# Zero rows and columns around a hybrid decoder step's small matrix products, and one exponent matrix per delta head

## The chip, the cores and the metric

The kernel runs on one core of one Trainium2 chip. The time is the device time of one execution, in microseconds (us); before the change it is 2520.16, the median of three runs (2520.1 to 2521.52).

## The reference

Two decoder layers run for a prompt of 512 tokens and for 8 samples of 8 new tokens each, with the same weights. Each layer projects the normalised input once, gives the columns to three branches, merges them by sigmoid gates, projects again, adds the residual, and ends with a gated MLP. The branches are HGRN2 (a gated linear recurrence), differential attention, and the gated delta rule. The delta rule is the one whose algebra the change touches; per chunk and head it is

```python
G = jnp.cumsum(gc, axis=-1)
D = jnp.exp(jnp.where(incl, G[..., :, None] - G[..., None, :], -jnp.inf))
KK = jnp.einsum('bhtd,bhsd->bhts', kc, kc)
A = jnp.where(strict, bc[..., :, None] * D * KK, 0.0)
eg = jnp.exp(G)[..., None]
rhs = bc[..., None] * (vc - eg * jnp.einsum('bhtd,bhdv->bhtv', kc, S))
U = lax.linalg.triangular_solve(A, rhs, left_side=True, lower=True, unit_diagonal=True)
QK = jnp.einsum('bhtd,bhsd->bhts', qc, kc) * D
o = eg * jnp.einsum('bhtd,bhdv->bhtv', qc, S) + jnp.einsum('bhts,bhsv->bhtv', QK, U)
S = jnp.exp(GL)[..., None, None] * S + jnp.einsum('bhsd,bhsv->bhdv', kc * jnp.exp(GL[..., None] - G)[..., None], U)
```

with `q`, `k` normalised to length 1 per token (and `q` divided by the root of 128), `b` the beta of a token, and an RMS norm of `o` over the head's 128 values behind it.

## The kernel before

All 576 tokens (512 of the prompt, 64 of the samples, `NS`) lie along the free dimension, 128 channels along the partitions. A projection's tile of 128 output channels is made by `dense_steps` (line 265): for each 128 input channels six products of 128x288 in the fp32r type (weight high with input high and low, weight low with input high, over two halves of the tokens). These big products accumulate in two PSUM tiles `acc`. For one output tile (`wide=True`, line 1420, the first output projection of layer 0) the halves are 512 and 64 tokens instead.

Everything else on TensorE is small: fp32 products (each shown as two instructions, two passes) and transposes (one instruction) of 128 tokens at a time, made by `mm` (line 180) and `trp` (line 190) into tiles of the pool `psR`, which has four PSUM banks and is shared by all heads (`rp`, line 169). The samples' 64 tokens are a fifth block, and most products on it have 64 rows or 64 columns of the array.

The order of the work is planned when the program is made. `drive` (line 319) keeps three lanes (left, right, samples). Each lane runs one head at a time as a Python generator; `yield win(i)` asks for a projection tile, `yield 0.7` lets the lane sleep for so long by a clock `clk` to which each product adds an assumed cost. Between the lanes' steps `drive` issues the big products of the next tile. The instructions of an engine then run in the order in which the program stands, except that one whose inputs come late in the framework's own plan may have been put behind others.

A delta head (`gdn_head`, line 752; 4 per layer) does the following. Convolution and SiLU of the keys and queries into `ckq` (`conv_silu`), transposition of the keys into `kt`, sums of squares `ss`. `parts(i)` splits an exponent per token into three bf16 parts `pc`; `weights(i, pc)` transposes them (15 columns), spreads them over the array with five selector products on 15 rows (`sel`, `rt`), adds the other exponent `w1` and a mask, takes the exponential into `dd`, and multiplies it into the products of keys with keys (i = 0) or keys with queries (i = 1), giving `ap[:, i]` for the prompt and `aps[:, i]` for the samples. `weights(0)` is called at line 835, the solve of the 16x16 diagonal blocks follows on VectorE with two round trips through DRAM and ends in `TB` and `TS`; after `yield 4.5` (line 886) comes `weights(1)`, then `yield 11.0` (line 907), and then products of `ap[:, 0]` and `TB` that build the whole inverse. The chunk loop makes `R`, `U` and the state `S`; the samples' part makes `Rs` and `Us` with 64x64 products. `sample_state` and `finish_gated` end the head; the latter uses `head_norm` and `transpose_back`.

`hgrn_head` (line 990) makes its matrix by levels m = 1, 2, ..., 64 (`level`, line 1026); for m up to 4 each has a product for the samples on 64 columns. Its samples' output starts with the 64x64 product of `ATs`. `diff_head` and `qk_prep` use `transpose_to` (line 470) and `transpose_back` (line 485); `diff_sample` multiplies the weights `PT` by past values and, for the samples' own tokens, by `Vs` on 64 rows.

Of the kernel before, what the change touches and what calls it, by code (L numbers as in the profile page):

```python
# [28 lines left out]
HALF = T // 2  # L29
PAST = 1024  # L30
# [115 lines left out]
def kernel(ctx, tc, a, o, depth=DEPTH, dbg=None):  # L146
# [118 lines left out]
    def dense_steps(src, xs, M=128, raws=None, nk=None, prime=False, wide=False):  # L265
# [23 lines left out]
        for g, (k0, n) in enumerate(gr):  # L289
            wh, wl = nxt  # L290
            for i in range(n):
                if i == min(1, n - 1) and g + 1 < len(gr):
                    nxt = weights(g + 1)
                xh, xl = xs[k]
                cs = slice(i * M, (i + 1) * M)
                for w, xx in ((wh, (xh, xl)), (wl, (xh,))):
                    for hf in range(2):
                        for x_ in xx:
                            ts = (slice(0, SEQ), slice(SEQ, T))[hf] if wide else slice(hf * HALF, (hf + 1) * HALF)
                            mm(acc[:M, hf, :ts.stop - ts.start], w[:, cs], x_[:, ts],  # L300
                               start=(k == 0 and w is wh and x_ is xh), stop=(k == nk - 1 and w is wl))
                k += 1
                if k < nk:
                    yield
        if wide:
            return acc.rearrange('p a b -> p (a b)')[:, 0:T].rearrange('p (a b) -> p a b', a=2)
        return acc[:, :, :HALF]

    def dense(src, xs, wide=False):
        return run(dense_steps(src, xs, wide=wide))  # L310
# [159 lines left out]
    def transpose_to(dst, src, scale=None):  # L470
# [4 lines left out]
        trp(ps2[:NS, 0:128], src[:, SEQ:], ident)  # L475
        G.memset(dst[NS:, 4, :], 0.0)
        if scale is None:
            S.copy(dst[:, 0:4, :], ps.rearrange('p (j d) -> p j d', j=4))
            S.copy(dst[:NS, 4, :], ps2[:NS, 0:128])
# [3 lines left out]
        S.activation(dst[:NS, 4, :], ps2[:NS, 0:128], AF.Copy, scale=scale[:NS, 4:5])  # L483

    def transpose_back(src):
# [18 lines left out]
    def finish_gated(ot, key, src, gcol, dst, p, tag):  # L504
# [3 lines left out]
        head_norm(ot, p)  # L508
# [128 lines left out]
    for l in range(depth):  # L637
# [10 lines left out]
        bh = lay.tile([128, 5, 4], F32, tag='bh', name='bh')  # L648
# [4 lines left out]
        GB = lay.tile([128, 5, 4], F32, tag='GB', name='GB')  # L653
        GC = lay.tile([128, 5, 4], F32, tag='GC', name='GC')
# [19 lines left out]
        def decays(p):  # L674
# [9 lines left out]
            S.activation(bh, sp[:, :, 0:4], AF.Exp, scale=-1.0)  # L684
            V.tensor_scalar(out=bh, in0=bh, scalar1=0.5, scalar2=None, op0=ALU.mult)
# [3 lines left out]
            lab = lay.tile([NS, NB, 4], F32, tag='lab', name='lab')  # L689
            tt(lab, bc1(la[:NS, 4, :], NB), bc(c['bm8'][:NS], 4), ALU.mult)  # L690
# [4 lines left out]
            mm(ps[:, 32:64], ones[:NS, :], lab.rearrange('p b e -> p (b e)'))  # L695
            mm(ps[:NS, 64:68], c['trib'][:NS], la[:NS, 4, :])
            mm(ps[:NS, 68:72], c['oneb'][:NS], la[:NS, 4, :])
# [6 lines left out]
            tt(GB, Gt, sp[:, :, 0:4], ALU.subtract)  # L704
            V.tensor_scalar(out=GC, in0=Gt, scalar1=-0.5 * math.log(128.0), scalar2=None, op0=ALU.add)
            V.tensor_scalar(out=nG, in0=Gt, scalar1=-1.0, scalar2=None, op0=ALU.mult)
# [45 lines left out]
        def gdn_head(h, p):  # L752
            ckq = p.tile([128, 2, T], F32, tag='ckq', name='ckq')
            cv = p.tile([128, T], F32, tag='hn', name='cv')
            sel = c['sel'].rearrange('p (j t) -> p j t', j=5)
            mad = c['madd'].rearrange('p (a t) -> p a t', a=2)
            mads = c['madds'].rearrange('p (a t) -> p a t', a=2)
            conv_silu((yield win(4 * h + 0)), 4 + h, ckq[:, 0])
# [5 lines left out]
            aps = p.tile([NS, 2, NS], F32, name='aps')  # L764
# [6 lines left out]
            trp(ps2[:NS, 0:128], ckq[:, 0, SEQ:], ident)  # L771
            S.copy(kt[:, 0:4], ps.rearrange('p (j t) -> p j t', j=4))
            S.copy(kt[:NS, 4], ps2[:NS, 0:128])
# [5 lines left out]
            u2 = sm.tile([128, 2, 5], F32, tag='u2', name='u2')  # L779
            V.scalar_tensor_tensor(out=u2[:, 0], in0=ss[:, 0], scalar=-0.5, in1=GB[:, :, h], op0=ALU.mult, op1=ALU.add)  # L780
# [3 lines left out]
            def parts(i):  # L784

                pc = sm.tile([128, 3, 5], BF16, tag='pc', name='pc')
                rr = sm.tile([128, 5], F32, tag='rr', name='rr')
                V.tensor_copy(pc[:, 0], u2[:, i])
                tt(rr, u2[:, i], pc[:, 0], ALU.subtract)
# [3 lines left out]
                return pc  # L793

            def weights(i, pc):
# [4 lines left out]
                V.tensor_copy(rt, pst[:15, 0:128])  # L800
                yield 0.7
                pb, pg = rp(), rp()
                for j in range(4):
                    cs = slice(128 * j, 128 * j + 128)
                    mm(pb[:, cs], sel[:15, j, :], rt)
                    mm(pg[:, cs], ckq[:, 0, cs], ckq[:, i, cs])
                dd = p.tile([128, 4, 128], F32, tag='x5', bufs=2, name='dd')
                for j in range(4):
                    V.scalar_tensor_tensor(out=dd[:, j], in0=pb[:, 128 * j:128 * j + 128], scalar=w1[:, j:j + 1], in1=mad[:, i],
                                           op0=ALU.add, op1=ALU.add)  # L810
                if i:
                    S.activation(eq[:, 0:SEQ], pb, AF.Exp)
# [5 lines left out]
                if i:  # L818
                    S.activation(eq[:, SEQ:], pb[:, 0:NS], AF.Exp)
                dds = p.tile([NS, 4, 16], F32, tag='dds', name='dds')  # L820
                dv = dds.rearrange('p j t -> p (j t)')
                V.scalar_tensor_tensor(out=dv, in0=pb[:NS, 0:NS], scalar=w1[:NS, 4:5], in1=mads[:NS, i], op0=ALU.add, op1=ALU.add)
                S.activation(dv, dv, AF.Exp)
                tt(aps[:, i], pb[:NS, 128:128 + NS], dv, ALU.mult)

            pc = parts(0)
            conv_silu(acc, h, ckq[:, 1])
            ex = sm.tile([128, 2, 5], F32, tag='ex', name='ex')
            V.tensor_copy(ex[:, 0], u2[:, 0])
# [5 lines left out]
            yield from weights(0, pc)  # L835
# [9 lines left out]
            tt(xts, aps[:, 0].rearrange('p (j t) -> p j t', j=4), bc(bm[:NS, 0:4], 16), ALU.mult)  # L845
# [20 lines left out]
            TS = p.tile([NS, 2, 4, 16], F32, name='TS')  # L866
            for i in range(2):
                for cc in range(4):
                    tt(TB[:, i, cc].rearrange('p (j t) -> p j t', j=8), bc1(ct[:, i, cc], 8), bc(bm, 16), ALU.mult)
                tt(TS[:, i], bc1(ct[:NS, i, 4], 4), bc(bm[:NS, 0:4], 16), ALU.mult)  # L870

            conv_silu(acc, 8 + h, cv)
            yield 1.0
            ps, ps2 = rp(), rp()
            for j in range(5):
                n = 128 if j < 4 else NS
                pj = ps[:, 128 * j:128 * j + 128] if j < 4 else ps2[:NS, 0:128]
                trp(pj, ckq[:, 1, 128 * j:128 * j + n], ident)
                ks = p.tile([128, 128], F32, tag='U', bufs=2, name='ks')
                S.activation(ks[:n], pj, AF.Square, accum_out=ss[:n, 1, j:j + 1])  # L880
            S.activation(ss[:, 1], ss[:, 1], AF.Ln, bias=b4e)
            V.scalar_tensor_tensor(out=u2[:, 1], in0=ss[:, 1], scalar=-0.5, in1=GC[:, :, h], op0=ALU.mult, op1=ALU.add)
            pc = parts(1)
# [731 lines left out]
```

## Time and profile before

| | |
|---|---|
| median of three runs | 2520.16 us |
| profiled execution, device time | 2517.85 us |
| its span, first to last instruction | 2516.1 us |
| TensorE busy with products | 2492.3 us (99%) |
| TensorE busy with weight loads | 2338.6 us (93%) |
| VectorE busy | 1677.5 us (67%) |
| ScalarE busy | 1134.2 us (45%) |
| GpSimd busy | 119.3 us (5%) |
| granted TensorE clock, mean | 0.999 |
| products on TensorE | 19714 |

The times of instructions come from one execution, the profiled one. In the page and the timeline a product is written `out<-moving,stationary`, then the rows and columns of the array that it takes (`64*128` is 64 rows and 128 columns), then its input's form. `r` is a tile of the pool `psR`, `acc` the accumulator of a big product, `cf` the constants (for a transpose, the identity). Products are pipelined: a row's duration reaches from its start to its end, and the next product starts well before that end.

### The profile page before, as it was taken

Reading aid. Unit: us, or ns where it says so; the run is one execution under the profiler, and the core shown is the slowest. Engines: PE = TensorE matmul, PEld = TensorE weight load, DVE = VectorE, ACT = ScalarE, POOL = GpSimd, SP = SyncE. Lnnn points to the kernel's source line nnn. Section 1 sums busy time; section 2 is a strip of 40 time slices with the busy share of each in tenths; the row PEclk is TensorE's granted clock in tenths of the full one; section 3 lists DMA queues with packets and bytes.
Section 4 is the critical chain, followed back from the end, with each engine's and each line's share of the span. In section 5 each row is a group of like instructions: output and inputs, shape, how many; then the busy total and the mean of one; then the engine's idle time right before and its main releaser. Section 6 shows DMA issues by size and latency. Waiting matters only on the chain.

```text
span 2516.1 us, 52047 instructions
## 1 busy us (share of the span) xinstructions
PE 2492.3 (99%) x19714; PEld 2338.6 (93%) x19714; DVE 1677.5 (67%) x4218; ACT 1134.2 (45%) x2435; POOL 119.3 (5%) x378
## 2 busy tenths in 40 slices
PE   8999999999999999999999999999999999999999
PEld 7898888888899999999998988888889999999999
DVE  7777777777765663646676877777686656636463
ACT  5556555556433332323455565646464333323232
POOL 1000000000000010101000000000000000101010
PEclk9999999999999999999999999999999999999999
DMA  6233464545365324242432235554534653242423
GB/s 206 88 109 120 141 202 133 181 156 177 104 213 173 133 85 159 85 146 95 137 130 95 96 121 181 168 176 148 180 129 160 192 176 119 86 159 82 159 85 124
DMA packets 222843, 352.93 MB, mean 140 GB/s; under 512 B 36864, under 2 KB 71680, under 8 KB 222592
## 3 DMA queue, kind: packets, MB, share of 16 engines
q1 hardware_dynamic: 221008, 346.78, 42.3%
q8 instruction: 156, 2.56, 0.4%
q10 hardware_dynamic: 1584, 2.82, 0.4%
q14 instruction: 95, 0.78, 0.1%
HBM read 288.90 MB, written 60.60 MB: 139 GB/s over the span
## 4 chain that ended last, share of the span: by engine, by line
PE 93%; DVE 4%; ACT 2%; issue 1%; DMA 0%; SPq 0%; ACTq 0%; DVEq 0%
PE acc L188 75%; PE r L188 14%; PE r L192 4%; DVE mx L1216 1%; DVE wl L195 0%; ACT P L1219 0%; DVE r L195 0%; DMA x<-in_xT 0%; DVE mx L1289 0%; DMA pg<-in_v 0%; ACT ks L777 0%; DVE ca L743 0%; DVE thb L723 0%; DVE xl L427 0%; DVE ro L195 0%
## 5 line engine op out<-in xcount | busy, mean ns | idle before, releaser
L188 PE MATMUL acc<-xh,wh 128*128 128x288 f32 x3584 | 1026.1, 301 | 2.9 <-DVE thb L710 1.6
L188 PE MATMUL acc<-xl,wh 128*128 128x288 f32 x3584 | 1010.7, 297 | 1.0 <-DVE xl L427 0.9
L188 PE MATMUL acc<-xh,wl 128*128 128x288 f32 x3584 | 773.3, 296 | 5.3 <-DVE wl L195 5.3
L262 ACT CAST wh<-raw 128x512 fp32r<-128x512 f32 x624 | 383.5, 615 | 841.0 <-PE acc L188 791.8
L188 PEld LDWEIGHTS acc<-xh,wh 128*128 128x128 f32 x3584 | 674.5, 188 | 33.8 <-issue 19.4
L188 PEld LDWEIGHTS acc<-xl,wh 128*128 128x128 f32 x3584 | 675.5, 188 | 6.4 <-issue 2.9
L188 PEld LDWEIGHTS acc<-xh,wl 128*128 128x128 f32 x3584 | 576.7, 188 | 11.9 <-DVE wl L195 6.5
L195 DVE TENSOR_TENSOR wl<-raw,wh 128x512 fp32r<-128x512 f32 x624 | 423.2, 679 | 187.7 <-ACT wh L262 183.7
L188 PE MATMUL acc<-hl,wh 128*128 128x288 f32 x704 | 197.5, 296 | 0.0
L188 PE MATMUL acc<-hh,wh 128*128 128x288 f32 x704 | 196.7, 294 | 0.0
L188 PE MATMUL acc<-hh,wl 128*128 128x288 f32 x704 | 150.7, 295 | 0.0
L188 PEld LDWEIGHTS acc<-hh,wh 128*128 128x128 f32 x704 | 132.2, 188 | 0.0
L188 PEld LDWEIGHTS acc<-hl,wh 128*128 128x128 f32 x704 | 132.0, 188 | 0.0
L188 PEld LDWEIGHTS acc<-hh,wl 128*128 128x128 f32 x704 | 113.9, 189 | 0.0
L188 PE MATMUL acc<-oL,wh 128*128 128x288 f32 x384 | 108.0, 295 | 0.0
L188 PE MATMUL acc<-oh,wh 128*128 128x288 f32 x384 | 107.3, 295 | 0.0
L195 DVE TENSOR_TENSOR cbf<-acc,rb 128x288 f32<-128x288 f32 x132 | 39.1, 352 | 90.2 <-PE acc L188 86.3
L1456 DVE SCALAR_TENSOR_TENSOR caf<-cbf,fm,caf 128x592 f32<-128x592 f32 x88 | 73.5, 835 | 15.1 <-ACT caf L1454 13.5
L188 PE MATMUL acc<-oh,wl 128*128 128x288 f32 x384 | 81.6, 293 | 0.0
L1412 DVE SCALAR_TENSOR_TENSOR xn<-acc,xo 128x576 f32<-128x576 f32 x40 | 30.3, 758 | 73.3 <-PE acc L188 73.3
L188 PEld LDWEIGHTS acc<-oL,wh 128*128 128x128 f32 x384 | 73.0, 190 | 0.0
L188 PE MATMUL acc<-mh,wh 128*128 128x288 f32 (+2 forms) x256 | 72.3, 296 | 0.0
(415 smaller groups left out, 3665.5 us busy)
## 6 DMA issues: line engine op xcount, KB each, us to landing
raw<-in_w_in_t SPq DMA_DIRECT2D x272, 256.0 KB
raw<-in_w_up SPq DMA_DIRECT2D x176, 256.0 KB
pg<-in_kT SPq DMA_DIRECT2D x128, 256.0 KB
pg<-in_v SPq DMA_DIRECT2D x128, 256.0 KB
raw<-in_w_dn SPq DMA_DIRECT2D x64, 256.0 KB
xo<-xres SPq DMA_DIRECT2D x56, 288.0 KB
thd<-thb SPq DMA_DIRECT2D x48, 288.0 KB
th<-thd SPq DMA_DIRECT2D x48, 288.0 KB
```

Source lines behind the costliest of these rows:

```text
L188: PE.matmul(out, lhsT, rhs, start=start, stop=stop, **kw)
L192: PE.transpose(out, in_, idm)
L195: (eng or V).tensor_tensor(out=out, in0=in0, in1=in1, op=op)
L262: S.copy(hi, src)
L1216: V.tensor_reduce(out=mx[:, cc:cc + 1], in_=pss[cc][:, :nk], axis=AX.X, op=ALU.max)
L1412: V.scalar_tensor_tensor(out=v2(xn), in0=acc, scalar=0.5, in1=v2(xo), op0=ALU.mult, op1=ALU.add)
L1456: V.scalar_tensor_tensor(out=A[:, 0:592], in0=P[:, j:j + 592], scalar=w[:, 3 * fi + j:3 * fi + j + 1], in1=A[:, 0:592], op0=ALU.mult, op1= ...
```

## The change

The diff does four things.

- Tiles that small products read get 128 tokens or rows in the samples' block, with zeros behind the 64 (`TP = SEQ + 128`; `ckq`, `cv`, `XX`, `xr`, `aps`, `TS`, `Rs`, `Us`, `ATs`, `Vs`, `P`, `lab`), cleared by GpSimd. The products and transposes on them then take 128 rows and 128 columns. `ATs` instead becomes two products on 32 columns each, as its neighbours are. Left as they are: the past attention's and the samples' state products on 32 columns or rows, the scores on 64 rows, level 64 and some of the norms' and decays' products.
- `weights` is called once per delta head. One exponent matrix serves keys and queries; the selector products have 128 rows and stand together ahead of the others; one product has keys and queries side by side as 256 moving columns. The query's norm leaves the matrix: it becomes a factor `cn` per token that `head_norm` applies.
- beta moves from the rows to the columns of the matrix, by `nG`, so that it lies in the keys (`w1`, and with it `ex[:, 1]`); `GB`, `GC` and `bh` are gone, and the values are scaled by 0.5 alone.
- `wide` is gone; all output tiles use two halves of 288 tokens.

The core of the diff:

```diff
-        trp(ps2[:NS, 0:128], src[:, SEQ:], ident)
-        G.memset(dst[NS:, 4, :], 0.0)
+        trp(ps2[:, 0:128], src[:, SEQ:], ident)
...
-        trp(ps2[:, 0:NS], src[:NS, 4, :], ident[:NS, :NS])
+        trp(ps2[:, 0:128], src[:, 4, :], ident)
...
-    def head_norm(ot, p):
+    def head_norm(ot, p, cn=None):
...
+        for _ in range(0 if cn is None else 2):
+            tt(ms, ms, cn, ALU.mult)
...
+        if cn is not None:
+            tt(r, r, cn, ALU.mult)
...
-            mm(ps[:, 32:64], ones[:NS, :], lab.rearrange('p b e -> p (b e)'))
-            mm(ps[:NS, 64:68], c['trib'][:NS], la[:NS, 4, :])
+            mm(ps[:, 32:64], ones, lab.rearrange('p b e -> p (b e)'))
+            mm(ps[:NS, 64:68], c['trib'], la[:, 4, :])
...
-                trp(pst[:15, 0:128], pc.rearrange('p a j -> p (a j)'), identb)
-                rt = sm.tile([15, 128], BF16, tag='rt', name='rt')
+                trp(pst[:, 0:128], pc, identb)
+                rt = sm.tile([128, 128], BF16, tag='rt', name='rt')
...
-                pb, pg = rp(), rp()
+                pb, pg = rp(), (rp(), rp())
+                for j in range(4):
+                    mm(pb[:, 128 * j:128 * j + 128], sel[:, j, :], rt)
                 for j in range(4):
                     cs = slice(128 * j, 128 * j + 128)
-                    mm(pb[:, cs], sel[:15, j, :], rt)
-                    mm(pg[:, cs], ckq[:, 0, cs], ckq[:, i, cs])
+                    mm(pg[j // 2][:, 256 * (j % 2):256 * (j % 2) + 256].rearrange('p (i t) -> p i t', i=2), ckq[:, 0, cs], ckq[:, :, cs])
...
-                tt(ap[:, i], pg.rearrange('p (j t) -> p j t', j=4), dd, ALU.mult)
+                S.activation(eq[:, 0:SEQ], pb, AF.Exp)
+                for g in range(2):
+                    for i in range(2):
+                        tt(ap[:, i, 2 * g:2 * g + 2], pg[g].rearrange('p (j i t) -> p i j t', j=2, i=2)[:, i], dd[:, 2 * g:2 * g + 2], ALU.mult)
                 pb = rp()
-                mm(pb[:, 0:128], sel[:15, 4, :], rt)
-                mm(pb[:NS, 128:128 + NS], ckq[:, 0, SEQ:], ckq[:, i, SEQ:])
+                mm(pb[:, 0:128], sel[:, 4, :], rt)
+                mm(pb[:, 128:256].rearrange('p (i t) -> p i t', i=2), ckq[:, 0, SEQ:], ckq[:, :, SEQ:T])
...
-            yield 4.5
-            yield from weights(1, pc)
...
-            for j in range(5):
-                n = 128 if j < 4 else NS
-                S.activation(bV[:n, j], ps[:, 128 * j:128 * j + 128] if j < 4 else ps2[:NS, 0:128], AF.Copy, scale=bh[:n, j, h:h + 1])
+            S.activation(bV[:, 0:4], ps.rearrange('p (j t) -> p j t', j=4), AF.Copy, scale=0.5)
+            S.activation(bV[:, 4], ps2[:, 0:128], AF.Copy, scale=0.5)
...
-            mm(pu[:NS, 0:128], TTs, Rs)
+            mm(pu[:, 0:128], TTs, Rs)
...
-            mm(pu[:NS, 0:128], aps[:, 1], Us)
+            mm(pu[:, 0:128], aps[:, NS:], Us)
...
-                    mm(ps[:NS, :NS], lhs[:, SEQ:], rhs[:, SEQ:])
+                    mm(ps[:, :NS], lhs[:, SEQ:], rhs[:, SEQ:T])
...
-                    mm(halves(ps[:NS, 0:NS // 2], m), lhs[:, SEQ:], second(rhs[:, SEQ:], m))
+                    mm(halves(ps[:, 0:NS // 2], m), lhs[:, SEQ:], second(rhs[:, SEQ:T], m))
...
-            mm(pu[:NS, 0:128], ATs, vt[:NS, 4], stop=False)
+            for q in range(2):
+                mm(pu[32 * q:32 * q + 32, 0:128], ATs[:, 32 * q:32 * q + 32], vt[:, 4], stop=False, tile_position=(0, 32 * q))
...
-                        mm(po[hs], PT[:NS, i, hs], Vs[:, h], start=False, stop=True, tile_position=(0, 32 * h))
+                        mm(po[hs], PT[:, i, hs], Vs[:, h], start=False, stop=True, tile_position=(0, 32 * h))
...
-                acc = dense(a['w_out'][l, f], mixs, wide=(l, f) == (0, 0))
+                acc = dense(a['w_out'][l, f], mixs)
```

## Rows read from the trace of the kernel before

**Rows 1.** The page's part 1: engine, busy us, share of the span, instructions.

```profile
PE 2492.3 (99%) x19714; PEld 2338.6 (93%) x19714; DVE 1677.5 (67%) x4218; ACT 1134.2 (45%) x2435; POOL 119.3 (5%) x378
```

**Rows 2.** TensorE's waits: us in total, times, longest us; the first row.

```profile
PE acc L188 <- DVE wl L195: 5.3, 4, 2.0
...
```

**Rows 3.** Timeline of TensorE: start, us, operation, number; two full passes between big products.

```profile
306.89 0.29 PE L188 MATMUL acc<-xl,wh 128*128 128x288 f32 x1
307.03 0.38 PE L188 MATMUL r<-bV,TB 128*128 128x128 f32 x2
...
307.38 0.29 PE L188 MATMUL acc<-xl,wh 128*128 128x288 f32 x1
```

**Rows 4.** The same view, two passes on 64 rows and 64 columns.

```profile
683.52 0.42 PE L188 MATMUL acc<-xh,wl 128*128 128x288 f32 x2
683.88 0.43 PE L188 MATMUL r<-Rs,TS 64*64 64x128 f32 x2
...
684.47 0.29 PE L188 MATMUL acc<-xl,wh 128*128 128x288 f32 x1
```

**Rows 5.** Groups by line and form, TensorE: the selector products.

```profile
L188 PE MATMUL r<-rt,cb_c 15*128 15x128 bf16 x80 | 16.9, 223 | 1.0 <-DVE rt L800 1.0
```

**Rows 6.** Timeline of TensorE, one call of `weights`: first and last products, next big one.

```profile
1727.24 0.22 PE L188 MATMUL r<-rt,cb_c 15*128 15x128 bf16 x1
...
1729.70 0.33 PE L188 MATMUL r<-ckq 128*64 128x64 f32 x2
...
1730.20 0.42 PE L188 MATMUL acc<-xh,wl 128*128 128x288 f32 x2
```

**Rows 7.** The same view, a call whose four selectors stand together.

```profile
1631.86 0.39 PE L188 MATMUL r<-rt,cb_c 15*128 15x128 bf16 x4
1632.19 1.16 PE L188 MATMUL r<-ckq 128*128 128x128 f32 x8
```

**Rows 8.** The same view, five transposes; the fifth has 64 rows, then 64 columns.

```profile
68.30 0.80 PE L192 MATMUL r<-cf,ro 128*128 128x128 f32 x5
...
69.27 0.30 PE L188 MATMUL acc<-xl,wh 128*128 128x288 f32 x1
...
270.11 0.71 PE L192 MATMUL r<-cf,cv 128*128 128x128 f32 x5
...
270.79 0.29 PE L188 MATMUL acc<-xl,wh 128*128 128x288 f32 x1
```

**Rows 9.** The same view, HGRN levels: eight full, two narrow passes; eight narrow passes.

```profile
279.63 1.23 PE L188 MATMUL r<-XX 128*128 128x64 f32 x10
...
281.16 0.29 PE L188 MATMUL acc<-xh,wh 128*128 128x288 f32 x1
...
658.15 0.68 PE L188 MATMUL r<-XX 128*64 128x64 f32 x8
658.76 0.40 PE L188 MATMUL acc<-xh,wl 128*128 128x288 f32 x1
```

**Rows 10.** The same view, one step of six products in halves of 512 and 64.

```profile
795.23 0.48 PE L188 MATMUL acc<-mh,wh 128*128 128x512 f32 x1
...
796.26 0.48 PE L188 MATMUL acc<-mh,wh 128*128 128x512 f32 x1
```

**Rows 11.** Timeline of VectorE and TensorE around one call of `weights`.

```profile
248.52 0.21 DVE L749 SCALAR_TENSOR_TENSOR ckq<-ct,ca 128x64 f32<-128x64 f32 x1
...
256.34 0.33 PE L188 MATMUL r<-ckq 128*64 128x64 f32 x2
256.60 0.66 PE L192 MATMUL r<-cf,P 128*128 128x128 f32 x4
...
259.22 0.69 DVE L195 TENSOR_TENSOR ap<-r,dd 128x512 f32<-128x512 f32 x1 [1.29 <-ACT dd L813]
```

**Rows 12.** The same two engines at the end of one block solve.

```profile
289.58 0.49 DVE L195 TENSOR_TENSOR TB<-ctt,cf 128x128 f32<-128x128 f32 x2
...
289.94 0.29 PE L188 MATMUL r<-TB,ap 128*128 128x64 f32 x1
```

More of the change, by code (lines that the diff above doesn't have):

```diff
@@ L29 @@
 HALF = T // 2
+TP = SEQ + 128
 PAST = 1024
@@ L304, in dense_steps, with dense @@
                     yield
-        if wide:
-            return acc.rearrange('p a b -> p (a b)')[:, 0:T].rearrange('p (a b) -> p a b', a=2)
         return acc[:, :, :HALF]
-    def dense(src, xs, wide=False):
-        return run(dense_steps(src, xs, wide=wide))
+    def dense(src, xs):
+        return run(dense_steps(src, xs))
     def run(g):
@@ L501, in head_norm, with finish_gated @@
         rsqrt(r, ms, 5)
+        if cn is not None:
+            tt(r, r, cn, ALU.mult)
         tt(ot, ot, bc(r, 128), ALU.mult)
-    def finish_gated(ot, key, src, gcol, dst, p, tag):
+    def finish_gated(ot, key, src, gcol, dst, p, tag, cn=None):
         yield ('fill', key)
@@ L507, in finish_gated @@
         nc.sync.dma_start(og, src)
-        head_norm(ot, p)
+        head_norm(ot, p, cn)
         yield 5.0
@@ L703, in decays @@
             S.activation(eGs, ps[:, 32:64].rearrange('p (j e) -> p j e', e=4), AF.Exp)
-            tt(GB, Gt, sp[:, :, 0:4], ALU.subtract)
-            V.tensor_scalar(out=GC, in0=Gt, scalar1=-0.5 * math.log(128.0), scalar2=None, op0=ALU.add)
-            V.tensor_scalar(out=nG, in0=Gt, scalar1=-1.0, scalar2=None, op0=ALU.mult)
+            V.scalar_tensor_tensor(out=nG, in0=Gt, scalar=-1.0, in1=sp[:, :, 0:4], op0=ALU.mult, op1=ALU.subtract)
         def half(dst, acc):
@@ L778, in gdn_head, with parts @@
             S.activation(ss[:, 0], ss[:, 0], AF.Ln, bias=b4e)
[L779 to L780 removed]
+            u2 = sm.tile([128, 5], F32, tag='u2', name='u2')
+            V.scalar_tensor_tensor(out=u2, in0=ss[:, 0], scalar=-0.5, in1=Gt[:, :, h], op0=ALU.mult, op1=ALU.add)
             w1 = sm.tile([128, 5], F32, tag='w1', name='w1')
             V.scalar_tensor_tensor(out=w1, in0=ss[:, 0], scalar=-0.5, in1=nG[:, :, h], op0=ALU.mult, op1=ALU.add)
[L784 to L786 removed]
+            def parts():
+                pt_ = sm.tile([128, 128], BF16, tag='pc', name='pc')
+                G.memset(pt_, 0.0)
+                pc = pt_[:, 0:15].rearrange('p (a j) -> p a j', a=3)
                 rr = sm.tile([128, 5], F32, tag='rr', name='rr')
[L788 to L789 removed]
+                V.tensor_copy(pc[:, 0], u2)
+                tt(rr, u2, pc[:, 0], ALU.subtract)
                 V.tensor_copy(pc[:, 1], rr)
@@ L818, in weights @@
-                if i:
-                    S.activation(eq[:, SEQ:], pb[:, 0:NS], AF.Exp)
+                mm(pb[:, 0:128], sel[:, 4, :], rt)
+                mm(pb[:, 128:256].rearrange('p (i t) -> p i t', i=2), ckq[:, 0, SEQ:], ckq[:, :, SEQ:T])
+                S.activation(eq[:, SEQ:], pb[:, 0:NS], AF.Exp)
                 dds = p.tile([NS, 4, 16], F32, tag='dds', name='dds')
                 dv = dds.rearrange('p j t -> p (j t)')
-                V.scalar_tensor_tensor(out=dv, in0=pb[:NS, 0:NS], scalar=w1[:NS, 4:5], in1=mads[:NS, i], op0=ALU.add, op1=ALU.add)
+                V.scalar_tensor_tensor(out=dv, in0=pb[:NS, 0:NS], scalar=w1[:NS, 4:5], in1=mads, op0=ALU.add, op1=ALU.add)
@@ L834, in gdn_head @@
             acc = yield win(4 * h + 2)
-            yield from weights(0, pc)
+            yield from weights(pc)
             cm = p.tile([128, 5, 16], F32, tag='cm', name='cm')
@@ L973, in gdn_head @@
                            tile_position=(0, g))
-            Rs = p.tile([NS, 128], F32, tag='R', name='Rs')
-            V.scalar_tensor_tensor(out=Rs, in0=pu[:NS, 0:128], scalar=nk[:NS, 4:5], in1=bV[:NS, 4], op0=ALU.mult, op1=ALU.add)
+            Rs = p.tile([128, 128], F32, tag='R', name='Rs')
+            G.memset(Rs[NS:], 0.0)
+            V.scalar_tensor_tensor(out=Rs[:NS], in0=pu[:NS, 0:128], scalar=nk[:NS, 4:5], in1=bV[:NS, 4], op0=ALU.mult, op1=ALU.add)
             S.copy(ot[:NS, 4], pu[NS:, 0:128])
@@ L1023, in hgrn_head @@
             AT = p.tile([128, 4, 128], F32, name='AT')
-            ATs = p.tile([NS, NS], F32, name='ATs')
+            ATs = p.tile([128, NS], F32, name='ATs')
+            G.memset(ATs[NS:], 0.0)
             def level(lhs, rhs, m):
@@ L1049, in level @@
                     ps = rp()
-                    mm(halves(ps[:NS, 0:NS // 2], m), lhs[:, SEQ:], second(rhs[:, SEQ:], m))
-                    V.copy_predicated(second(ATs, m), second(c[f'u{m}'][:NS, :NS], m), halves(ps[:NS, 0:NS // 2], m))
-            e2 = lambda t: t.rearrange('p (n e) -> p n e', e=2)
+                    mm(halves(ps[:, 0:NS // 2], m), lhs[:, SEQ:], second(rhs[:, SEQ:T], m))
+                    V.copy_predicated(second(ATs[:NS, :NS], m), second(c[f'u{m}'][:NS, :NS], m), halves(ps[:NS, 0:NS // 2], m))
+            e2 = lambda t: t[:, 0:T].rearrange('p (n e) -> p n e', e=2)
             X, Y, rf = flip(), flip(), f2('lf')
@@ L1276, in diff_sample @@
                 mm(sn[32 * h:32 * h + 32, 0:NS], Qs[:, b, h, :], kTs[:, h], tile_position=(0, 32 * h))
-            tt(P[:, PAST:], sn[:, 0:NS], c['smask'][:, NS * b:NS * b + NS], ALU.add)
-            V.tensor_reduce(out=mx[:, 2:3], in_=P[:, PAST:], axis=AX.X, op=ALU.max)
+            tt(P[:, PAST:PAST + NS], sn[:, 0:NS], c['smask'][:, NS * b:NS * b + NS], ALU.add)
+            V.tensor_reduce(out=mx[:, 2:3], in_=P[:, PAST:PAST + NS], axis=AX.X, op=ALU.max)
             Vp = []
```

135 lines of the change are left out of this document (68 added, 67 removed).

## The prediction

> **What bounds the kernel now.** I read the page's engine line first: TensorE is busy 2492.3 of the span's 2516.1 us [rows 1]. Busy need not mean needed, so the second view is TensorE's waits: twelve rows, the largest 5.3 us in all [rows 2]. So TensorE's own stream of products sets the end, and what counts is how far each product pushes the next one back. That is not the duration in a row (0.29 us for a big product); it is the distance between starts, and the third view, the timeline of TensorE, has it. Big products (128x288, 14736 of them by the loops of the code) start 0.13 us apart; small products sit between them in groups.
>
> I price a group as the time from the start of the last big product before it to that of the second one after it, less two steps of 0.132 us. A pair of 128x128 passes (one fp32 product is two passes) costs 306.89 to 307.38 less 0.264, 0.23 us, or 0.112 a pass [rows 3]. The two passes of `Rs`, 64 rows by 64 columns of the array, cost 683.65 to 684.47 less 0.264, 0.56 us [rows 4]; the row at 683.52 holds two products, the second at 683.65. They do less work and cost 0.33 us more: the entry takes 0.23 instead of 0.13 us, the second pass comes no sooner, and the next big product starts 0.20 us behind it instead of 0.03. I call this the price of changing the array's shape; it falls on every group whose rows or columns don't fill the array.
>
> **The change part by part.**
>
> *A. The exponent products of the delta heads* (`weights`, called twice per head, 16 times). Now five bf16 selector products on 15 rows (80 in all [rows 5]) alternate with fp32 products on 128 rows. One call runs from 1727.24 to the second big product at 1730.20, 2.96 us [rows 6]; with the entry of 0.23 and less 0.264 it costs 2.92. In two of the calls the four selectors came out side by side: four within 0.33 us and the eight passes after them in 1.16 us [rows 7], so such a call costs about 2.0, 0.9 less for three changes of shape less. Sum now 14 x 2.92 + 2 x 2.0 = 44.9 us. Each call also has a transpose with 15 columns alone between big products; no row prices it, and I take the 0.33 of a change of shape: 16 x 0.35 = 5.6. After: one call per head; five selectors on all rows at 0.056 (the spacing in [rows 7], that is between nothing and the 0.112 of an fp32 pass), eight passes of 256 columns, taken as twice 0.112 each, and two for the samples: 0.28 + 1.79 + 0.22 = 2.3, and a full transpose of 0.11. Eight heads: 19.3. **Gain 31.2 us** (29 with the dear selectors).
>
> *B. Transposes back* (`transpose_back`, 4 heads x 4 x 2 layers = 32 calls). Four full ones and one of 64 rows take 68.30 to 69.27, 0.97 us; four full ones and one of 64 columns take 270.11 to 270.79, 0.68 us [rows 8]. A full fifth costs what the latter does, so 32 x 0.29 = **9.2 us**. The same rows say that the padding in `transpose_to` and of the delta heads' three other transposes brings nothing: a transpose of 64 columns already costs no change of shape.
>
> *C. `Rs` and `Us`*, 16 products: 16 x 0.33 = 5.3. Their operand comes from VectorE or ScalarE just before, and part of the dear entry covers that wait (up to 0.09 us each): **4.6 us** (between 3.8 and 5.3).
>
> *D. Sample tails of the HGRN levels* (m = 1, 2, 4; 24 products). Eight full passes and two on 64 columns run from 279.63 to the third big product at 281.16: 1.53 + 0.13 - 0.396 = 1.27 [rows 9]; ten full passes cost 1.12. 24 x 0.15 = **3.6 us**. Against it stands that narrow passes are closer: eight on 64 columns take 0.61 us with the exit [rows 9], eight full ones 0.90. So padding pays for groups of up to four or five passes; the change leaves the groups of eight narrow. The Trainium skill ("TensorE: Matmul & The Clock Gate", section LDWEIGHTS) says that a weight load takes as long as it has columns, whatever its rows; by that alone every 64-column product here gets dearer. This trace agrees for long runs and not for pairs, where the change of shape outweighs it.
>
> *E. The sample values' products* (16 in the past attention) and `ATs` (8) lie beside products on 32 columns and so lose one of two changes: half of 0.33, less the added passes, 24 x 0.13 = **3.2 us**. *F.* The first output projection goes from 512+64 to 288+288 columns: a step of six products took 795.23 to 796.26, 1.03 us [rows 10], against 6 x 0.132 = 0.79: 8 x 0.24 = **1.9 us**. *G.* `decays`: one change less in each layer, **0.3 us**.
>
> *Costs.* The new `weights` takes five PSUM tiles in a row where the pool has four, and ends with all four in use. The products' readers trail: the last product of a call starts at 256.34, the `ap` product on VectorE, which frees the bank, is done at 259.91 [rows 11]. A small product of another lane right behind must wait for the oldest bank, read by four VectorE instructions and one ScalarE exponential; these can now start 1.8 us before the call ends, since the selectors come first. Between nothing and 3.3 us per call; I take 0.25 x 8 = **2 us**, near the lower end, since big products, which have banks of their own, mostly come between. The key-query products now need the query's convolution as well: its last write ended at 248.73, five microseconds ahead of the products [rows 11], so nothing. What follows on VectorE and ScalarE gets less (one exponent matrix instead of two, five evictions become two). The added clears go to GpSimd, 5% busy [rows 1], several microseconds ahead of their readers: nothing, or as much as the next clear is late, since GpSimd works in order. The rows `rt` among the waits may shrink: **-1 us**.
>
> Sum: 31.2 + 9.2 + 4.6 + 3.6 + 3.2 + 1.9 + 0.3 - 2 + 1 = 53 us. The profiled execution took 2517.85, which gives 2464.9; the median of the runs is 2.3 higher, 2520.16, so I forecast **2467 us**.
>
> **The rivals.**
> 1. *Banks.* If every call is followed at once by another lane, eight stalls of up to 3.3 us take back 26 us: 2480 to 2493. For it: the call of [rows 11] is followed at once by four transposes. Against: readers start earlier than now.
> 2. *The type also counts.* Selectors are bf16 between fp32 products, so part of their price could be the change of type. Each call would keep two changes, each transpose one: 8 x 3 x 0.33 = 7.9 us less, 2475. Against: the fp32 `Rs` pays the full price without a change of type.
> 3. *Padding doesn't fill the array*: if the price came from something that zeros leave in place (the operands' own size), only the halving of `weights` stays, 25 us, and the banks: 2495. The skill's rule on columns would add 0.05 us for each widened pass to this case, some 5 us, 2500. Against: [rows 3, 4].
> 4. *Slower: the block solve.* The second call and its hold (`yield 4.5`, then 0.7) stood between the solve of the 16x16 blocks and its first product, `ap` times `TB`. If the product moves ahead with the plan, TensorE stops in front of it in order, with all big products behind it, by up to 4.5 + 0.7 + 2.9 + 0.35 = 8.5 us per head: 68 us, 2532. From 6.6 us per head on it eats the gain. Against: that product now starts at 289.94, 0.36 us behind the first write of `TB` at 289.58 [rows 12], so it already stands where its input comes, not where the holds would put it.
>
> **How the numbers follow.** Forecast 0.67 (2456 to 2478: selectors at 0.056 or 0.112, the wait in C, rival 2's half, four microseconds of changed waits); banks 0.17; type 0.06; no filling 0.05; solve 0.05, of which 0.03 end slower. The range reaches from 2456 to 2488: it takes in forecast, type and half of the banks, 0.8 in all. A measurement of this kernel tells 0.2% (5 us) from no change. Faster 0.96, same 0.01, slower 0.03.
>
> **What would show it.** In the timeline of TensorE after: the four selectors at some 0.06 us side by side and eight passes of 0.21 to 0.22 behind them, one call of 2.3 us per head (A; rival 2 if the first pass comes 0.15 late); five transposes in 0.68 us (B); `Rs` and `Us` at 0.23 to 0.32 (C); no row of TensorE's waits over 6 us. I am wrong if the small products keep their entries of 0.23 and exits of 0.20 us, if TensorE's waits grow past 20 us (banks, solve), or if big products no longer start every 0.13 us.

## The result, and the profile after

The changed kernel takes 2458.89 us (median; the kernel before beside it 2520.84), a ratio of 0.9753 with the interval 0.9736 to 0.977. The forecast was 2467, 2456 to 2488. Part 1 of the page after answers to [rows 1]: 112 products fewer, and TensorE as full as before.

```profile
PE 2434.7 (99%) x19602; PEld 2311.1 (94%) x19602; DVE 1667.2 (68%) x4156; ACT 1124.5 (46%) x2401; POOL 129.0 (5%) x442
```

TensorE's waits after, the view of [rows 2] (us in total, times, longest us). No wait took the place of the work: the largest is about the one of before, the next are small, and the view's rows sum to 18.9 us in both kernels.

```profile
PE acc L189 <- DVE wl L196: 4.9, 6, 1.9
PE acc L189 <- DVE XX L704: 2.0, 2, 1.0
PE r L193 <- DVE ln_r L255: 1.9, 3, 0.6
PE r L193 <- DVE ot L196: 1.6, 4, 0.5
...
PE r L189 <- DVE TB L196: 0.6, 2, 0.4
```

The timeline of TensorE after (start, us, operation, number; `mm` is line 189 there, `trp` 193) shows the new forms: one call of `weights`, the two passes of `Rs` where their operand was ready, and a transposition back.

```profile
366.77 0.40 PE L189 MATMUL r<-rt,cb_c 128*128 128x128 bf16 x4
367.00 1.95 PE L189 MATMUL r<-ckq 128*128 128x256 f32 x8
368.79 0.22 PE L189 MATMUL r<-rt,cb_c 128*128 128x128 bf16 x1
...
369.25 0.29 PE L189 MATMUL acc<-xl,wh 128*128 128x288 f32 x1
...
546.19 0.29 PE L189 MATMUL acc<-xh,wh 128*128 128x288 f32 x1
546.32 0.39 PE L189 MATMUL r<-Rs,TS 128*128 128x128 f32 x2
...
546.68 0.29 PE L189 MATMUL acc<-xh,wh 128*128 128x288 f32 x1
...
69.75 0.71 PE L193 MATMUL r<-cf,ro 128*128 128x128 f32 x5
...
70.43 0.29 PE L189 MATMUL acc<-xl,wh 128*128 128x288 f32 x1
```

Four selectors take 0.23 us, where before one came every 0.58, the eight passes of 256 columns 1.79, and the call 2.48 to the second big product behind it (369.25), against 2.96 for one of two calls [rows 6]. `Rs` costs 546.19 to 546.68 less 0.264, 0.23 us, against 0.56 [rows 4]. The five transposes take 0.68 to the second big product, as four with a fifth of 64 columns did, and not the 0.97 of a fifth with 64 rows [rows 8].

But a table by stage, from the first product of each stage in the two timelines, shows a gain where nothing was changed:

| stage (both layers) | before, us | after, us | gain |
|---|---|---|---|
| heads, from the start to the first product on `oh` | 717.07 + 700.09 | 694.25 + 678.34 | 44.6 |
| branch projections | 76.18 + 76.17 | 76.17 + 76.17 | 0.0 |
| output projection (`mh`) | 53.04 + 50.58 | 50.57 + 50.57 | 2.5 |
| gated MLP to the next layer or the end | 419.45 + 423.50 | 414.31 + 418.42 | 10.2 |

The spans differ by 57.3 us: 10 of them are the MLP, whose code is the same. One of its stretches, 56 steps of six big products on the hidden values `hh`, begins and ends with these products, first before, then after:

```profile
1087.66 0.29 PE L188 MATMUL acc<-hh,wh 128*128 128x288 f32 x1
...
1132.46 0.29 PE L188 MATMUL acc<-xh,wh 128*128 128x288 f32 x1
```

```profile
1060.58 0.29 PE L189 MATMUL acc<-hh,wh 128*128 128x288 f32 x1
...
1104.26 0.29 PE L189 MATMUL acc<-xh,wh 128*128 128x288 f32 x1
```

44.80 us are 800 ns a step, 43.68 are 780. The granted clock is 1.00 in both stretches. So there are two questions: whether the price of a change of shape is what the small products gained, and what shortened the MLP.

### The profile page after: what moved, and what is told of

Read it like the earlier page. It is cut to its first block, busy times and chain, and to the rows that moved or that the text cites. A ratio compares the mean times of both kernels' runs of the same rounds, so it can differ in the third digit from the quotient of the medians.

```text
span 2458.8 us, 51886 instructions
## 1 busy us (share of the span) xinstructions
PE 2434.7 (99%) x19602; PEld 2311.1 (94%) x19602; DVE 1667.2 (68%) x4156; ACT 1124.5 (46%) x2401; POOL 129.0 (5%) x442
## 4 chain that ended last, share of the span: by engine, by line
PE 91%; DVE 5%; ACT 1%; issue 1%; DMA 1%; SPq 0%; ACTq 0%; DVEq 0%
PE acc L189 74%; PE r L189 13%; PE r L193 4%; DVE mx L1222 1%; DVE wl L196 1%; DVE dtr L196 0%; DVE s L527 0%; ACT P L1225 0%; DVE r L196 0%; DMA x<-in_xT 0%; DMA ctt<-dt 0%; DVE rs_w L259 0%; DVE ot L196 0%; ACT ks L773 0%; DMA dt<-dtr 0%
## 5 line engine op out<-in xcount | busy, mean ns | idle before, releaser
L1463 DVE SCALAR_TENSOR_TENSOR caf<-cbf,fm,caf 128x592 f32<-128x592 f32 x88 | 73.5, 835 | 15.1 <-ACT caf L1461 13.5
L189 PEld LDWEIGHTS acc<-oh,wh 128*128 128x128 f32 x384 | 72.1, 188 | 0.0
```

Of the source, the lines that this page charges most:

```text
L189: PE.matmul(out, lhsT, rhs, start=start, stop=stop, **kw)
L1463: V.scalar_tensor_tensor(out=A[:, 0:592], in0=P[:, j:j + 592], scalar=w[:, 3 * fi + j:3 * fi + j + 1], in1=A[:, 0:592], op0=ALU.mult, op1= ...
```

## The experiments

Each was run beside the kernel before, whose medians were 2518.24 to 2520.92; ratios are to it.

**1. The selectors' rows alone** (kernel before, two calls per head).

```diff
-                pc = sm.tile([128, 3, 5], BF16, tag='pc', name='pc')
+                pt_ = sm.tile([128, 128], BF16, tag='pc', name='pc')
+                G.memset(pt_, 0.0)
...
-                    mm(pb[:, cs], sel[:15, j, :], rt)
+                    mm(pb[:, cs], sel[:, j, :], rt)
```

> The kernel before with one part of the change alone: the exponents' parts, their transposed tile and the five selector products take 128 rows instead of 15 (zeros behind them). Still two calls per head, selectors still alternate with fp32 products, the last fp32 product of a call stays on 64 columns. The start of the MLP's tiles is kept where it was. Theory (the price is the change of the array's shape, 0.33 us): a call falls from 2.92 (2.0 in two of them) to 5 x 0.056 + 8 x 0.112 + 0.56 = 1.74 us, 16 calls together -17 us, and the transposes of 15 columns 16 x 0.24 = -4 us: 2520.5 - 21 = 2500 us, the selectors' first pass in a call no longer late. Rival (the change of type between bf16 and fp32 costs as much as the change of shape): the alternation goes on costing, no gain, 2520; half and half 2510.

Measured 2502.65 us, ratio 0.9937 (0.9921 to 0.9954): 15.6 us less.

**2. Their order alone** (kernel before, 15 rows).

```diff
                 pb, pg = rp(), rp()
+                for j in range(4):
+                    mm(pb[:, 128 * j:128 * j + 128], sel[:15, j, :], rt)
...
-                    mm(pb[:, cs], sel[:15, j, :], rt)
```

> The kernel before with the other part alone: the four selector products of a call stand together ahead of the four key-query products, still on 15 rows, still two calls per head. Theory (changes are paid, not products): three changes of shape less in the 14 calls that alternate, 0.9 us each: 2520.5 - 13 = 2508 us, and a call starts like the rows of the two calls that came out so before (four selectors in 0.33 us, eight passes in 1.16 us). Rival (each product on 15 rows costs its extra time wherever it stands): 2520. If both this run and the one with full selectors gain as forecast, their gains must not add up: they remove the same changes.

Measured 2503.64, ratio 0.9937 (0.992 to 0.9953): 14.6 us less.

**3. Both.**

> The kernel before with both halves of the new selector products: 128 rows instead of 15, and the four of a call side by side ahead of the key-query products; still two calls per head. Alone, full rows gave 15.6 us and the order 14.6 us. Theory (both remove the same changes of shape): a call costs 5 x 0.056 + 8 x 0.112 + 0.56 = 1.74 us, the alternation of types (some 0.02 us each) is gone too; 16 calls from 2.83 to 1.74 and the transposes' 2.4 us: -20 us, 2498 to 2500 us. Rival (two separate costs, that of a narrow product and that of alternation): the gains add up, -30 us, 2488.

Measured 2497.64, ratio 0.9908 (0.9893 to 0.9922): 22.9 us less, against the 30 of the sum. The same call of `weights` (key-query products, then narrow ones of another lane) in the timelines of TensorE, first in the kernel before, then with full rows, with the new order, and with both:

```profile
372.34 0.22 PE L188 MATMUL r<-rt,cb_c 15*128 15x128 bf16 x1
...
372.92 0.23 PE L188 MATMUL r<-rt,cb_c 15*128 15x128 bf16 x1
...
375.06 0.32 PE L188 MATMUL r<-kTs,Qs 128*32 128x64 f32 x8
```

```profile
369.95 0.23 PE L191 MATMUL r<-rt,cb_c 128*128 128x128 bf16 x1
370.02 0.44 PE L191 MATMUL r<-ckq 128*128 128x128 f32 x2
370.30 0.22 PE L191 MATMUL r<-rt,cb_c 128*128 128x128 bf16 x1
...
371.70 0.32 PE L191 MATMUL r<-kTs,Qs 128*32 128x64 f32 x8
```

```profile
374.24 0.39 PE L188 MATMUL r<-rt,cb_c 15*128 15x128 bf16 x4
374.56 1.16 PE L188 MATMUL r<-ckq 128*128 128x128 f32 x8
...
376.07 0.32 PE L188 MATMUL r<-kTs,Qs 128*32 128x64 f32 x8
```

```profile
372.25 0.40 PE L191 MATMUL r<-rt,cb_c 128*128 128x128 bf16 x4
372.48 1.11 PE L191 MATMUL r<-ckq 128*128 128x128 f32 x8
...
373.83 0.32 PE L191 MATMUL r<-kTs,Qs 128*32 128x64 f32 x8
```

Before, this call took 2.72 us from its first selector to the products behind it; it takes 1.75, 1.83 and 1.58. Each part alone takes away most of the same cost, so what is paid is the change and not the product. The type is a small part: with full rows, selector and two fp32 passes alternate every 0.33 to 0.35 us, where 0.06 and 0.22 stand for the work, so the two changes of type (to bf16 and back) cost about 0.06 us together. With 15 rows the same round took 0.58, so the two changes of shape in it cost about 0.3. Rival 2 is out, but for that remainder. The run with both gained 22.9 where 20 were forecast, no more of a difference than medians can tell.

**4. The hidden tiles 128 bytes further up** (kernel before). The program places `hh` and `hl` at 123264 and on; each is 2304 bytes, nine times 256, so all of them start 128 behind a multiple of 256. In the changed kernel other tiles have other sizes, and they start at 123648, a multiple of 256.

```diff
     gt = pool('gt', bufs=2)
+    padp = pool('padp', bufs=1)
...
+    pad = padp.tile([128, 32], F32, tag='pad', name='pad')
+    nc.gpsimd.memset(pad, 0.0)
```

> The kernel before, with every tile of the head stages on the left side, of the mixed stream and of the MLP's hidden values 128 bytes further up in SBUF (an unused tile of 128 bytes below them); no other instruction changed. The profiled pair shows the MLP 5.1 us shorter in each layer after the change, though its code is the same: before, the hidden tiles start 128 bytes behind a multiple of 256 and six products of a step take 790 to 800 ns; after, they start on a multiple of 256 and a step takes 780. Theory (where a moving tile starts sets the spacing of big products): steps of 780 ns in the MLP here too, -10 us, 2510 us, the head stages unchanged. Rival (the spacing follows from the stream of instructions ahead, or is luck of an execution): 2520, steps of 790 to 800 as before.

Measured 2508.52, ratio 0.9963 (0.9949 to 0.9978): 9.7 us less.

**5. and 6. The same in the changed kernel**, by 128 bytes and (the same edit with 16 columns) by 64.

> The changed kernel with the same tiles 128 bytes further up, so that the hidden tiles start 128 bytes behind a multiple of 256 as they did in the kernel before. Theory (start of the moving tile): MLP steps go from 780 to 790 to 800 ns, +10 us, 2469 us, and the change itself is then worth 51 us at equal placement. Rival (stream or luck): 2459.

> The changed kernel with the left side's tiles 64 bytes further up: hidden tiles 64 bytes behind a multiple of 256. With 128 bytes the MLP's steps went from 780 to 790 and 800 ns, and the branch outputs, 224 bytes behind, always run at 793. Theory (only a multiple of 256 lets a step run at 780): steps of 785 to 800 ns on the hidden tiles and on the input tiles read behind them, +6 to +11 us, 2465 to 2470 us. Rival (a multiple of 64 is enough, 128 was a special case): 780, 2459 us.

Measured 2469.59, ratio 0.981 (0.9793 to 0.9826), and 2472.39, ratio 0.9806 (0.979 to 0.9822): 10.7 and 13.5 us more than the changed kernel. In run 4 the two MLP stages took 414.3 and 418.4 us, as in the changed kernel, without any of its other parts. The stretch shown above, in runs 4, 5 and 6:

```profile
1087.17 0.29 PE L191 MATMUL acc<-hh,wh 128*128 128x288 f32 x1
...
1130.85 0.29 PE L191 MATMUL acc<-xh,wh 128*128 128x288 f32 x1
```

```profile
1059.73 0.29 PE L192 MATMUL acc<-hh,wh 128*128 128x288 f32 x1
...
1104.53 0.29 PE L192 MATMUL acc<-xh,wh 128*128 128x288 f32 x1
```

```profile
1062.87 0.29 PE L192 MATMUL acc<-hh,wh 128*128 128x288 f32 x1
...
1107.67 0.29 PE L192 MATMUL acc<-xh,wh 128*128 128x288 f32 x1
```

43.68, 44.80 and 44.80 us: 780 ns a step where the tiles start on a multiple of 256, 800 where they start 128 or 64 behind one, in either kernel. The two kernels have different instructions ahead of the MLP and agree at equal placement, so the placement decides here. That settles the MLP: its 10 us are a by-product of the changed tile sizes. (In the profiles 64 bytes cost 2.4 us more than 128, since the first stretch of each layer and the output projection ran at 800 instead of 790.)

**7. The fifth transpose back on 64 rows** (changed kernel).

```diff
-        trp(ps2[:, 0:128], src[:, 4, :], ident)
+        trp(ps2[:, 0:NS], src[:NS, 4, :], ident[:NS, :NS])
```

> The changed kernel with the fifth transpose of each transposition back on 64 rows again, as before the change; the rest as changed. By the prediction's price this part is worth 32 x 0.29 = 9.2 us: 2468 us. By the accounts of the two traces half of it was lost, since the four gated heads' transposes of each branch now stand where they wait for their operand (four in 0.44 us where it is ready, entries of 0.2 to 0.8 us where it is not), and the change of shape is hidden in such a wait: 5 to 6 us, 2464 us. If the fifth transposes brought nothing: 2459.

Measured 2466.91, ratio 0.9788 (0.9774 to 0.9802): 8.0 us more.

```profile
68.33 0.80 PE L193 MATMUL r<-cf,ro 128*128 128x128 f32 x5
69.06 0.40 PE L189 MATMUL acc<-xh,wh 128*128 128x288 f32 x1
69.30 0.29 PE L189 MATMUL acc<-xl,wh 128*128 128x288 f32 x1
```

0.97 us again, 0.29 more than in the changed kernel. My expectation that a wait ahead of the group hides the change was mostly wrong. One group that comes 0.59 us behind the big product ahead in either kernel, since it waits for `ot`, costs 1.32 with the narrow transpose and 1.03 without: the change comes behind the wait and is paid in full. Five of the six groups of `ot` that come late behind a big product say the same; the sixth costs 1.28 in both, since in the changed kernel it waits 0.29 longer.

**8. The samples' products narrow again** (changed kernel).

```diff
-                    mm(ps[:, :NS], lhs[:, SEQ:], rhs[:, SEQ:T])
+                    mm(ps[:NS, :NS], lhs[:, SEQ:T], rhs[:, SEQ:T])
...
-                        mm(po[hs], PT[:, i, hs], Vs[:, h], start=False, stop=True, tile_position=(0, 32 * h))
+                        mm(po[hs], PT[:NS, i, hs], Vs[:NS, h], start=False, stop=True, tile_position=(0, 32 * h))
```

The other levels' product and `ATs` likewise.

> The changed kernel with the samples' products of the HGRN levels m = 1, 2, 4 on 64 columns again, and the samples' own value products of the past attention and ATs on 64 rows again, as before the change. The prediction's price: 24 x 0.15 + 24 x 0.13 = 6.8 us, 2466 us. By the accounts of the two traces: the level products 4.4 us and the value products 2.2 us dearer, ATs 1.0 us cheaper (its two products on 32 columns cost more than the one on 64), 5.6 us in all, 2464 us. If these groups are hidden by waits as I thought of the fifth transposes: 2459 to 2461.

Measured 2464.17, ratio 0.9781 (0.9766 to 0.9796): 5.3 us more. The two intervals touch, so the rows have to say it: ten passes of level 1, narrow tail first, then in the changed kernel.

```profile
382.74 1.32 PE L189 MATMUL r<-XX 128*128 128x128 f32 x10
383.99 0.40 PE L189 MATMUL acc<-xl,wh 128*128 128x288 f32 x1
```

```profile
382.22 1.24 PE L189 MATMUL r<-XX 128*128 128x128 f32 x10
383.27 0.38 PE L189 MATMUL acc<-xl,wh 128*128 128x288 f32 x1
```

1.25 against 1.05 us to the next big product. Summed over all groups, the levels are 3.3 us dearer with the narrow tails, the sample values 2.2; `ATs` is 0.9 cheaper and its neighbours 1.0 dearer, nothing together. (In these sums each product is charged the distance from the start before it, an entry less a step of 0.132, and the last of a group what its exit takes; so what a long product takes is charged to whatever stands behind it.)

**9. Longer sleeps ahead of the late operands** (changed kernel). Where `Rs` and `Us` wait for their operand they cost up to 0.70 us, and the transposes back of a gated head up to 1.28. One of these in the changed kernel, TensorE first, then VectorE:

```profile
668.24 0.74 PE L193 MATMUL r<-cf,ot 128*128 128x128 f32 x5 [0.54 <-DVE ot L196]
```

```profile
667.00 0.17 DVE L196 TENSOR_TENSOR ln_r<-ln_r,cn 128x5 f32<-128x5 f32 x1
667.27 0.83 DVE L196 TENSOR_TENSOR ot<-ot,ln_r 128x640 f32<-128x640 f32 x1
```

`head_norm` ends at 668.10 with the scaling of `ot`, with one more factor `cn` ahead of it (and two earlier), and TensorE stands for it. In the kernel before, the delta heads' transposes came 0.13 us behind a big product, or right behind other products; now six of the eight groups come late, by up to 0.70, 2.4 us in all. How much of it is `cn` and how much the faster TensorE, no run separates.

```diff
-        yield 5.0
+        yield 8.0
...
-            yield 0.8
+            yield 2.0
...
-            yield 0.7
+            yield 2.0
```

> The changed kernel with three longer sleeps of a lane: 8.0 instead of 5.0 ahead of the gated heads' transposes back, 2.0 instead of 0.8 and 0.7 ahead of the two sample products Rs and Us. In the changed kernel's trace Rs and Us cost 0.23 us where their operand is ready and up to 0.70 where TensorE stands for it, the five transposes 0.55 where ready and up to 1.28. Theory (what parts B and C lost are waits for the operand): these groups fall to 0.23 and 0.55, -5 us (8 x 0.2 for Rs and Us, 8 x 0.4 for the transposes, and less ahead of the others): 2453 to 2455 us. Rival (the plan only moves the standing elsewhere): no change, 2459, entries as long at other products.

Measured 2463.47, ratio 0.9772 (0.976 to 0.9785): no gain. The small products did fall by 5.6 us (all groups summed as above, 502.1 to 496.5; `Rs` and `Us` from 9.0 to 4.9, the transposes of `ot` from 18.1 to 15.4; of the 4.1 at `Rs` and `Us` only 1.2 are waits for the operand, and 2.1 come from four fewer `Rs` behind products of 512 columns, whose 0.52 us are charged to them), but the head stages stayed as long, 1373.6 us against 1372.6. The wait moved to the big products, as the rival has it. TensorE's first wait, one of its stops, and VectorE ahead of it:

```profile
PE acc L189 <- DVE XX L704: 9.1, 4, 2.6
```

```profile
364.71 0.29 PE L189 MATMUL acc<-xl,wh 128*128 128x288 f32 x1
367.60 0.40 PE L189 MATMUL acc<-xh,wh 128*128 128x288 f32 x1 [2.60 <-DVE XX L704]
```

```profile
364.40 0.17 DVE L196 TENSOR_TENSOR cn<-ss 128x5 f32<-128x5 f32 x1 [1.09 <-ACT ss L881]
...
366.80 0.75 DVE L704 SCALAR_TENSOR_TENSOR XX<-acc,rb 128x576 f32<-128x576 f32 x1
```

VectorE evicts the accumulator in the order of its program, here behind other work, a delta head's `cn` among it, which waits 1.09 us for ScalarE (the kernel before reads `ss` at that place too). The wait for XX grew by 7.1 us; 5.6 were won.

**10. to 12. Sleeps and the branch outputs' placement.** `oh` starts 224 bytes behind a multiple of 256 in both kernels; an unused tile moves it onto one.

```diff
                 brs.append((oh, ol))
+                if i == 11:
+                    G.memset(pmix.tile([128, 56], F32, name='ohpad'), 0.0)
```

> The kernel with the longer sleeps, and in the merge of the branches an unused tile of 224 bytes, so that the branch outputs oh start on a multiple of 256 bytes instead of 224 behind one. Theory (start of the moving tile): the 192 steps of the branch projections go from 793 to 780 ns, -2.5 us, and the 132 of the output projection behind them, which start on a multiple of 256 already but run at 790, too if they only carry on the rhythm that they enter with, -1.3 us: 2 to 4 us below the run with the longer sleeps alone. If only the MLP's tiles matter: no difference.

> The changed kernel with the longer sleeps of 2.0 ahead of Rs and Us alone, and oh on a multiple of 256 bytes. The run with all sleeps took 5.6 us off the small products and gave it back at the big ones: twice TensorE stood 2.6 us for an accumulator that VectorE had not yet evicted (XX), which the changed kernel did not do. Theory (the sleep of 8.0 shifted the plan of the next heads; the sleeps at Rs and Us did not): no stop of 2.6 us, Rs and Us at 0.23, 4 us less there and 2 to 4 us less by placement: 2453 to 2455. Rival (any shift of the plan brings such stops): 2457 to 2460.

> The changed kernel with middle sleeps (6.0 ahead of the gated heads' transposes, 1.4 ahead of Rs and Us) and oh on a multiple of 256 bytes. Theory: the operands now come in time (they were late by up to 0.7 us) and no accumulator waits: 2452 to 2455 us. Rival (any shift of the plan brings such stops): 2457 to 2460, with waits for XX over 5 us.

Measured 2460.66 (ratio 0.976, 0.9747 to 0.9773), 2460.21 (0.9769, 0.975 to 0.9789) and 2456.77 (0.9747, 0.9734 to 0.9761). The first is 2.8 us under the run with the sleeps alone, as expected, but their intervals overlap too. With the sleeps at `Rs` and `Us` alone TensorE stood 6.3 us for XX, longest 3.1, where I expected none. The middle sleeps (waits for XX 1.8 us) gave the lowest median, 2 us under the changed kernel, but the intervals overlap: not shown to be faster. In the run with sleeps at `Rs` and `Us` the first products on `oh`, then on `mh`, then on `xh` behind them, first layer and second:

```profile
695.53 0.29 PE L189 MATMUL acc<-oh,wh 128*128 128x288 f32 x1
...
770.41 0.29 PE L189 MATMUL acc<-mh,wh 128*128 128x288 f32 x1
...
820.33 0.29 PE L189 MATMUL acc<-xh,wh 128*128 128x288 f32 x1
...
1915.16 0.30 PE L189 MATMUL acc<-oh,wh 128*128 128x288 f32 x1
...
1992.61 0.30 PE L189 MATMUL acc<-mh,wh 128*128 128x288 f32 x1
...
2044.23 0.30 PE L189 MATMUL acc<-xh,wh 128*128 128x288 f32 x1
```

96 steps on `oh` take 74.88 us, 780 ns each, in the first layer and 77.45, 807 each, in the second, and the 64 on `mh` (128 in both layers, not the 132 expected) carry on at 780 and 807. In the other two runs `oh` ran at 790 (75.84), but for the second layer of the run with all sleeps, 780. At 224 behind, it was 76.17 to 76.45 in all the kernels, 793 to 796. So a start on a multiple of 256 lets a stretch run at 780, but it keeps the rhythm with which it is entered.

## Why the prediction was right, and where it was not

The time fell into the range, 8 us under the forecast, and partly by luck, for a reason that was not in it. The MLP gave 10.2 us by placement. Without that luck the time would still have been in the range: run 5, the change at the old placement, took 2469.59, 2.6 above the forecast. The change itself is worth 57.3 - 10.2 = 47.1 us in the profiled pair; runs at equal placement say 48.7 (2518.24 against run 5) and 49.6 (run 4 against 2458.89), and the medians less the 10.2 say 51.8. The forecast of 53 was 1 to 6 too high. Its steps:

- *The price of a change of shape* holds: 0.33 at `Rs` [rows 4], 0.29 at the transposes (run 7), 0.15 to 0.23 at the HGRN tails between big products (run 8), and runs 1 to 3 show that it hangs on the neighbours. That it falls on every group that doesn't fill the array was too wide: a transpose of 64 columns shows none [rows 8]. The Trainium skill ("TensorEngine Tiling (Array Packing)", section Key Properties) says that a change of the tiling mode drains TensorE, without a price. The runs agree that a change costs time, and give the price; that it is a drain, no run shows.
- *A*: 29.2 of 31.2 us (groups summed as in run 8: key-query products 28.60 to 15.66, selectors 16.64 to 4.53, their transposes 6.21 to 2.05). Selectors at 0.056 apart was the right bound. The halving of the calls has no run of its own; the whole change less runs 3, 7, 8 and *F* leaves 8 to 13 us for it, *C* and *G*.
- *B*: 8.0 by its removal, of 9.2. Against the kernel before only 5.9 show (`ro` 4.6, `ot` 1.3), mainly since the delta heads' transposes of `ot` now wait 2.4 us longer. This is the step that the runs show short: its price holds, but the sum has no term for that wait nor for `cn`, though `head_norm` is what these transposes stand for.
- *C*: 1.2 of 4.6 by these sums, which mislead here: they charge `Rs` with the 0.52 us of a product of 512 columns ahead of it, in six places now and in two before. Groups that stand alone between big products cost 0.58 us before (eleven) and 0.40 after (eight); with that gain for all, 16 x 0.18 = 2.9 us, still under the range of 3.8 to 5.3. The price was right (0.33 less per product with a ready operand). The wait of 0.09 us each was not: `Us` comes 0.25 us behind a big product in two places and 0.50 in two more, where it stands for ScalarE; a ready one comes at 0.13. With longer sleeps the waits of both fall from 1.3 to 0.1 us; the total doesn't follow (run 9). No run makes these two products alone narrow again, so how far this step fell short stays open.
- *D*: 4.4 of 3.6 (3.3 by removal). *E*: the values 2.2, `ATs` nothing, of 3.2: two products on 32 columns have more passes, which used up the change that they save. *F*: 8 steps from 1.03 to 0.79, 1.9, as said, and 0.6 more, since the 56 steps behind them go from 800 to 790 ns (in run 5 too). *G*: 0.2.
- *Costs and rivals.* No row of TensorE's waits names a reader of a `weights` call (`ap`, `dd`), where I took off 2 us for the banks; rival 1 is out. The 1 us for `rt` came: its row in that view (1.0 us) is gone. Rival 3 is out by every padded group. Rival 4: the product of `TB` waits 0.6 us in all. The parts sum to 45.6 of the 47.1 us.
- *"Big products every 0.13"* stood among the signs of error, as a number too coarse: 780 or 800 ns for six is 0.130 or 0.133; on all 14784 of them that would be 49 us, as much as the change itself.

## What to carry to other kernels

On a TensorE that is full, find each narrow product between full ones and price it by the starts around it; pad it, or put it beside its like, and expect the gain once. Where its operand has just been made, the producer can take part of the gain back, and here a longer sleep only moved the wait to what came later on VectorE. And compare the stages that the change doesn't touch: tile sizes move every tile behind them, so repeat the kernel before with the new placement before a gain is put down to the change.

## What the runs showed of the hardware

- Where a moving fp32r tile starts in SBUF changes the spacing of 128x288 products (runs 4 to 6). On a multiple of 256 bytes six products take 780, 790 or 807 ns, by the rhythm that they come in with; 64 behind one about 800, 128 behind 790 to 800, 224 behind 793 to 796. The input tiles, always on a multiple of 256, ran at 780 behind aligned hidden tiles and at 790 behind the others (87.36 against 88.48 us for 112 steps). A few small products in between can change the rhythm: the first input stretch of each MLP enters at 790, runs at 807 and then at 780 in both kernels. Why is open. The Trainium skill ("SBUF — State Buffer", section Operand start alignment) says of its own rule on starts that it is about legality and not speed; these runs show a cost of 1 to 3%.
- The small tiles of the heads don't show it: with those of the left side 128 bytes further up, the two head stages took 1417.8 us against 1417.2 in the kernel before, and 1369.9 against 1372.6 in the changed one. The 2.7 us less lie in the first layer, where the changed kernel's granted clock fell to 0.50 (1.2 GHz) from 28.3 to 35.1 us, after TensorE had been busy for 20.4 of 23.9 us, and that of run 5 stayed at 1.00.
- Going from fp32 to bf16 products and back costs some 0.06 us, a fifth of the 0.3 that going to 15 rows and back costs (run 1).
